# Tokens woven over partitions in steps of two, and longer runs in the DRAM turns, in a one-layer hybrid decoder

## The chip, the cores and the metric

The kernel runs on one core of one Trainium2 chip, in a single launch. The metric is the time of that launch on the device in microseconds (us); a lower one is better. The kernel before took 1533.48 us, the median of three runs that spread from 1532.01 to 1534.3.

## The reference

One decoder layer over 256 tokens of 2048 channels, in float32. Cut to what matters here:

```python
h = rmsnorm(x, norm_mix_w)                              # 256 x 2048
q, k, v, z, b, a, p_in, g_a, g_b = split(h @ w_in)      # 16 heads of 128
q, k, v = silu(causal_dwconv(concat(q, k, v), conv_w))  # 4 taps over tokens, one filter per channel
o = gated_delta_rule(l2norm(q), l2norm(k), v, g(a), sigmoid(b))
y_a = rmsnorm(o) * silu(z)
y_b = (multiscale_pool(p_in) @ pool_w) * pool_scale     # trailing means over 2, 4, 8, 16 tokens
x = x + (sigmoid(g_a) * y_a + sigmoid(g_b) * y_b) @ w_out
h = rmsnorm(x, norm_ffn_w)
gate, up = split(h @ w_up)                              # 2 x 5632 columns
gate = causal_dwconv(gate, conv_ffn_w) + conv_ffn_b     # 3 taps over tokens
x = x + (gelu(gate) * up) @ w_down
return rmsnorm(x)
```

## The kernel before

**The products.** `gemm_a` (line 356) computes 256 tokens by 512 columns. The activations are the loaded (stationary) operand, 128 channels by 128 tokens; the weights stream past them, 512 columns at a time. Activations and weights are each held as two float32r halves (`xhi`, `xlo`; `whi`, `wlo`), and a block is the sum of hi·hi, lo·hi and hi·lo. So a weight tile (`raw`, 256 channels by 512 columns, 512 KB) takes 12 matmuls: 8 with its `whi`, 4 with its `wlo`. The activations are `xhl` in the first half (q, k, v, pooled input, z and the two gates), `mhi`/`mlo` before the output projection, `fhl` before gate and up, `hhi`/`hlo` before the down projection. A block leaves in PSUM with tokens on partitions: `ps[:, t, :]` holds tokens 128t to 128t+127. `evict` (line 667) and `evicted` (line 1224) scale it by each token's norm factor (`rs1`, `rs2`: one number per partition and half) into a buffer `ev` or `fev`.

**The weight pipeline.** SyncE (its queue is called SP) loads the raw tile into one of five buffers, ScalarE (ACT) rounds it to `whi` (`cast`), VectorE (DVE) forms `wlo` (`split`). `whi` and `wlo` have four buffers each, so ACT and DVE can be at most about three tiles ahead of TensorE (PE). A raw tile is loaded when the split five tiles earlier is done.

**Turning a block.** The convolutions and the pooling run along tokens, so tokens must lie along the free dimension. `flip` (line 376) transposes 32x32 blocks on DVE (`tn`), writes them with four DMAs into a DRAM tensor `d` [512 channels, 256 tokens], and `flipped` loads that back with channels on partitions (`kq`, `vT`, `pu`, `gs`, `us`, ...). A 32x32 block row is 32 tokens, so a contiguous run in DRAM is 32 elements, 128 bytes. `flip` is used for k, q, v and the pooled input of each of four groups of heads, for the mixed output of each group (`sz` to `mhi`/`mlo`), for the four residual blocks (`xt` to `fhl`), and for 11 gate and 11 up blocks. `flip_back` (line 398) takes v back to tokens on partitions (`tb`, `back`, `vt`), again in runs of 32.

**The order.** Nothing is scheduled by hand or by the compiler: side work is written as generators ("threads"), and a planner (`Plan`, line 32) that keeps an estimated time for each engine decides after every few matmuls which thread moves on. `piece` picks a step when its operands are due, `pipeline` a load, a cast or a split. The DMA estimate (line 55) sets due times, 170 bytes per ns for runs of 32 elements and 380 for others. So a change of an estimate, or of the number of instructions of a step, moves instructions on all engines. Engines then execute in that fixed order.

**The groups.** Four groups of four heads pass through the first half, overlapped: the small products of a group's delta rule (`gdn`, line 718) are put between the weight matmuls of its gates and of the next group. The ones that matter below: from tile `lb`, 31 steps on DVE give `tb`, which goes through DRAM (`tbd`) to `tct`; then PE (`psa<-T,ga`), ACT (`U`) and DVE (`T`, `TT`) alternate. DVE also forms the trailing sums of the pooled input (`pb`, `pa` from `pu`). After the last group, its mixed output is transposed (`tn<-sz`), turned through DRAM, and split into `mhi` and `mlo`; three blocks of the output projection start on the channels of the first groups (`early`, line 1154, 18 weight tiles), and then PE needs the last group's `mhi` and `mlo`.

Of the kernel before, what the change touches and what calls it, by code (L numbers as in the profile page):

```python
# [13 lines left out]
P = 128  # L14
S = 256
# [16 lines left out]
class Plan:  # L32
# [75 lines left out]
def kernel(  # L108
# [264 lines left out]
        return ps  # L373


    def flip(pool, src, of, rank):
        yield "V", -2
        yield from take("tn")
        b = pool.tile([P, 2, 512], F32, tag="tn", name=nm("tn"))
        if of is None:  # L380
            for t in range(2):
                nc.vector.transpose(b[:, t, :], src[:, t, :])
        else:
            nc.vector.transpose(b.rearrange("p t f -> p (t f)"), src.rearrange("p t f -> p (t f)"))
            give(of)
        yield "S"
        d = dpool.tile([512, S], F32, tag="flip", bufs=4, name=nm("flip"))
        dv = d.rearrange("(f i) (t a j) -> a i t f j", i=32, t=2, j=32)
        for a in range(4):
            nc.sync.dma_start(dv[a], b[32 * a : 32 * a + 32].rearrange("p t (f j) -> p t f j", j=32))  # L390
        give("tn")
        yield "S", rank
        return d

    def flipped(dst, d):
        nc.sync.dma_start(dst, d.rearrange("(f p) s -> p f s", p=P))

    def flip_back(pool, src, dst, of):
        yield "V"
        yield from take("tn")  # L400
        b = pool.tile([P, 4, S], F32, tag="tn", name=nm("tb"))
        nc.vector.transpose(b.rearrange("p h s -> p (h s)"), src.rearrange("p h s -> p (h s)"))
        give(of)
        yield "S"
        d = dpool.tile([S, 512], F32, tag="back", name=nm("back"))
        dv = d.rearrange("(n i) (h a j) -> a i h n j", i=32, h=4, j=32)
        for a in range(4):
            nc.sync.dma_start(dv[a], b[32 * a : 32 * a + 32].rearrange("p h (n j) -> p h n j", j=32))
        give("tn")
        yield "S"  # L410
        nc.sync.dma_start(dst.rearrange("p t h d -> p t (h d)"), d.rearrange("(t p) c -> p t c", p=P))

    mix = tc.tile_pool(name="mix", bufs=1)
    mp = mix.__enter__()
# [66 lines left out]
    def xl(k, t):  # L481
        return xlo[:, k, t * P : (t + 1) * P]

    NV = 16 + KF
    V_FFN, V_CB = 0, 16
    vec = cpool.tile([P, NV], F32, name="vec")
# [3 lines left out]
    dtb = mp.tile([P, NH], F32, name="dtb")  # L490
    gwb = mp.tile([P, P], F32, name="gwb")
    rs1 = cpool.tile([P, 2], F32, name="rs1")
    rsh = cpool.tile([P, 2], F32, name="rsh")
    mats = mp.tile([P, 5, P], F32, tag="TT", name="mats")
    low, tri, ntri, ntail, top = (mats[:, i, :] for i in range(5))
# [15 lines left out]
    def norms():  # L511
        ssq4 = cpool.tile([P, 2, 4], F32, tag="ssq4", name="ssq4a")
        for c in range(4):
            for t in range(2):
                yield "A"
                plan.at(max(plan.ready, x0[c][1]))
                junk = cpool.tile([P, 512], F32, tag="sqj", name=nm("junk"))
                nc.scalar.activation(junk, x0[c][0][:, t, :], AF.Square, accum_out=ssq4[:, t, c : c + 1])
        yield "V"
        ssq = cpool.tile([P, 2], F32, name="ssq")  # L520
        nc.vector.tensor_reduce(ssq, ssq4, axis=mybir.AxisListType.X, op=ALU.add)
        rstd(ssq, rs1)
        normed.append(True)
        yield "V"
        nc.vector.tensor_scalar(rsh, rs1, 0.5, None, op0=ALU.mult)

    def vectors():
        yield "A"
# [189 lines left out]
    def gdn(g, kq, vts, dec0, dec1, res):  # L718
# [85 lines left out]
        nc.gpsimd.memset(TTa, 0.0)  # L804
        while not vts:
            yield
        vt = vts[0]
# [29 lines left out]
        for t in range(2):  # L837
            yield "A"
            for h in range(4):
                nc.scalar.activation(vt[:, t, h, :], vt[:, t, h, :], AF.Copy, scale=nk[:, t, h : h + 1])  # L840
        yield "PE"
        px = []
        for hp in range(2):
# [36 lines left out]
        w2 = mp.tile([P, 4, P], F32, tag="w2", name=nm("w2"))  # L880
        pw = pa([P, 4, P])
        for h in range(4):
            mm(pw[:, h, :], TT[h // 2][:, 0, h % 2, :], vt[:, 0, h, :], start=True, stop=True)
        yield "A"
        nc.scalar.copy(w1, pw)
        yield "PE"
# [4 lines left out]
        nc.vector.tensor_tensor(vt[:, 1], vt[:, 1], pr, op=ALU.subtract)  # L891
        yield "PE"
        pw = pa([P, 4, P])
        for h in range(4):
            mm(pw[:, h, :], TT[h // 2][:, 1, h % 2, :], vt[:, 1, h, :], start=True, stop=True)
        give("vt")
        yield "A"
        nc.scalar.copy(w2, pw)
# [109 lines left out]
    def mixing(g, sz, ps, psb, tb, res, mh, ml):  # L1008
        yield "V"
        nc.vector.scalar_tensor_tensor(tb, tb, 1.0, ps, op0=ALU.add, op1=ALU.mult)  # L1010
        yield "V"
        nc.vector.tensor_tensor(tb, tb, psb.unsqueeze(1).to_broadcast([P, 2, 512]), op=ALU.mult)
        give("psb")
        while len(res) < 2:
            yield
        plan.at(max(plan.ready, res[1]))
        yield "V"
        nc.vector.tensor_tensor(sz, sz, tb, op=ALU.add)
        give("th")
        d = yield from flip(mp, sz, "sz", g)  # L1020
        raw = ml.bitcast(F32)
        flipped(raw, d)
        yield "A"
        nc.scalar.copy(mh, raw)
        yield "V"
        nc.vector.tensor_tensor(ml, raw, mh.bitcast(F32), op=ALU.subtract)

    def gates(g):
        e = evict(gemm_a(xh, xl, KD))
# [34 lines left out]
    for g in range(4):  # L1064
# [33 lines left out]
        def values(e, g=g, vts=vts):  # L1098
            d = yield from flip(mp, e, "ev", g)
            yield from take("vT")  # L1100
            vT = mp.tile([P, 4, S], F32, tag="vT", bufs=1, name=nm("vT"))
            yield from conv_silu(d, 2, g, vT)
            yield "V"
            yield from take("vt")
            vt = mp.tile([P, 2, 4, P], F32, tag="vt", name=nm("vt"))
            yield from flip_back(mp, vT, vt, "vT")
            vts.append(vt)
            vts.append(plan.ready)

        if g == 0:  # L1110
            for k2 in range(8):
                plan.at(x0[k2 // 2][1])
                spawn(x_turned(k2), k2 - 20)

            def x_next(c):
                until(lambda: len(turned) > c)
                if c == 0:
# [8 lines left out]
            ps = gemm_a(xh, xl, KD, before=x_next)  # L1126
            pba = pa([P, 2, S])
            for c in range(2):
                hi, lo = weights()
                for kk in range(8):  # L1130
                    k = 8 * c + kk
                    mm(pba, hi[:, kk, :], xhl[:, k], start=(k == 0), stop=(k == KD - 1))
                side()

            def start(pba=pba, heads=heads):
                yield from strengths(pba)
                yield from heads()
        else:
            ps = gemm_a(xh, xl, KD)
        spawn(keys(evict(ps)), g)  # L1140
        if g == 0:
            spawn(start(), -1)
        spawn(queries(evict(gemm_a(xh, xl, KD))), g)
        if g:
            spawn(heads(), g)
        spawn(values(evict(gemm_a(xh, xl, KD))), g)
        if g:
            gates(g - 1)
    gates(3)
# [14 lines left out]
    ssq4 = cpool.tile([P, 2, 4], F32, tag="ssq4", name="ssq4b")  # L1164
    ssq2 = cpool.tile([P, 2], F32, name="ssq2")
    rs2 = cpool.tile([P, 2], F32, name="rs2")

    high = []
    squared = []

    def residual(c, ps):
# [5 lines left out]
        else:  # L1177
            nc.vector.tensor_tensor(xs, xs, ps, op=ALU.add)
        spawn(squares(c, xs), 0)
        d = yield from flip(fp, xs, None, 0)  # L1180
        ks = slice(4 * c, 4 * c + 4)
        raw = flo[:, ks, :].bitcast(F32)
        flipped(raw, d)
# [11 lines left out]
    def squares(c, xs):  # L1195
# [5 lines left out]
        if len(squared) == 4:  # L1201
            yield "V"
            nc.vector.tensor_reduce(ssq2, ssq4, axis=mybir.AxisListType.X, op=ALU.add)
            rstd(ssq2, rs2)
            squared.append(4)

    for c in range(4):
# [5 lines left out]
        spawn(residual(c, ps), 0)  # L1213

    def fh(k, t):
        return fhi[:, k, t * P : (t + 1) * P]

    def fl(k, t):
        return flo[:, k, t * P : (t + 1) * P]

    def fh_made(c):
        until(lambda: len(high) > c // 2)
# [1 line left out]
    def evicted(ps):  # L1224
# [2 lines left out]
        take_now("fev")  # L1227
        e = fp.tile([P, 2, 512], F32, tag="ev", name=nm("fev"))
        for t in range(2):
            nc.scalar.activation(e[:, t, :], ps[:, t, :], AF.Copy, scale=rs2[:, t : t + 1])  # L1230
        return e

    hhi = []
# [192 lines left out]
```

## Time and profile before

| what | value |
|---|---|
| median of three runs | 1533.48 us (1532.01 to 1534.3) |
| the profiled execution: its time, its span | 1536.53 us, 1533.5 us |
| mean granted TensorE clock in it | 0.997 |
| busy in the span: DVE, ACT, POOL | 69%, 51%, 4% |
| HBM read, written | 315.40 MB, 29.39 MB |
| DMA packets, of these under 512 B | 399271, 231190 |

The profile shows one execution, engine by engine. Its own time is 1536.53 us, of which 1533.5 are the span from the first to the last instruction; the profiled execution is 3.05 us longer than the median of the runs. In rows of the profile a name such as `psm<-whi,xhl` gives what an instruction writes and reads; PEld is the loading of the stationary operand, which overlaps PE's matmuls; SPq is SyncE's issuing of DMAs. Line 94 is a helper through which all instructions are recorded, so groups are told apart by tile.

### The profile page before, as it was taken

The page shows a single profiled execution, that of the slowest core. Times are in us where ns is not written, and L with a number is a line of the kernel's source. Part 1 is how long each engine was busy: PE and PEld are TensorE (multiplying, and loading weights), DVE is VectorE, ACT ScalarE, POOL GpSimd, SP SyncE. Part 2 cuts the span into 40 slices and gives each one's busy share as a digit, 9 for nine tenths or more (in the row PEclk, how much of TensorE's full clock was granted, in tenths as well). Part 3 has the DMA queues.
Part 4 walks back from the last instruction along what each step waited for, and adds up shares of the span by engine and source line. Part 5 has one row for each costly group of instructions (what it writes and reads, how often), then busy time and mean ns, then how long its engine had stood idle before and what let it go on. Part 6 is the DMA issues. An engine that isn't in the chain of part 4 may idle for free.

```text
span 1533.5 us, 19655 instructions
## 1 busy us (share of the span) xinstructions
PE 1519.9 (99%) x7110; PEld 1250.0 (82%) x7110; DVE 1059.4 (69%) x1525; ACT 775.4 (51%) x1023; POOL 62.5 (4%) x85
## 2 busy tenths in 40 slices
PE   9999999999999999999999999999999999999997
PEld 8887888777878887888888888888888888888886
DVE  5767878787887779885566766666666666444445
ACT  7475474466545854464455544444454444333343
POOL 1001001100010002000000000000000000000000
PEclk9999999999999999999999999999999999999999
DMA  8888975898578966974798888877887788666663
GB/s 292 224 238 219 256 243 149 206 260 256 159 178 245 288 201 167 264 230 143 228 281 270 235 255 245 258 220 242 253 248 227 237 255 240 204 193 192 220 194 108
DMA packets 399271, 346.09 MB, mean 226 GB/s; under 512 B 231190, under 2 KB 258374, under 8 KB 399174
## 3 DMA queue, kind: packets, MB, share of 16 engines
q1 hardware_dynamic: 395744, 339.32, 75.3%
q10 hardware_dynamic: 3430, 5.53, 1.1%
q8 instruction: 55, 0.90, 0.2%
q14 instruction: 42, 0.34, 0.1%
HBM read 315.40 MB, written 29.39 MB: 225 GB/s over the span
## 4 chain that ended last, share of the span: by engine, by line
PE 93%; DMA 3%; DVE 2%; issue 1%; SPq 0%; ACT 0%; POOLq 0%; POOL 0%; ACTq 0%; DVEq 0%
PE psm L94 79%; PE psa L94 8%; PE psb L94 6%; DMA raw<-in_w_in_dram 2%; DVE wlo L94 1%; DMA lb<-cdd 0%; DMA pu<-flip 0%; SPq L94 0%; DVE tmp L94 0%; ACT whi L94 0%; DVE tb L94 0%; DMA flip<-tn 0%; ACT xt L94 0%; DVE pb L94 0%; DVE tn L94 0%
## 5 line engine op out<-in xcount | busy, mean ns | idle before, releaser
L94 DVE TENSOR_TENSOR wlo<-raw,whi 128x1024 fp32r<-128x1024 f32 x524 | 635.2, 1220 | 293.1 <-ACT whi L94 291.4
L94 ACT CAST whi<-raw 128x1024 fp32r<-128x1024 f32 x526 | 549.0, 1051 | 536.9 <-PE psm L94 360.7
L94 PE MATMUL psm<-whi,xhl 128*128 128x512 f32 x1792 | 452.7, 393 | 1.4 <-ACT whi L94 1.4
L94 PEld LDWEIGHTS psm<-whi,xhl 128*128 128x128 f32 x1792 | 335.4, 188 | 71.6 <-ACT whi L94 2.2
L94 PE MATMUL psm<-whi,fhl 128*128 128x512 f32 x1408 | 347.8, 389 | 0.0
L94 PEld LDWEIGHTS psm<-whi,fhl 128*128 128x128 f32 x1408 | 264.5, 188 | 54.7
L94 PE MATMUL psm<-wlo,xhl 128*128 128x512 f32 x896 | 243.4, 394 | 0.6 <-DVE wlo L94 0.6
L94 PEld LDWEIGHTS psm<-wlo,xhl 128*128 128x128 f32 x896 | 167.4, 188 | 35.6 <-DVE wlo L94 1.1
L94 PE MATMUL psm<-wlo,fhl 128*128 128x512 f32 x704 | 188.3, 389 | 0.0
L94 PEld LDWEIGHTS psm<-wlo,fhl 128*128 128x128 f32 x704 | 132.2, 188 | 27.3
L94 PE MATMUL psm<-whi,hhi 128*128 128x512 f32 x168 | 65.4, 389 | 0.0
L94 PE MATMUL psm<-whi,hlo 128*128 128x512 f32 x168 | 65.4, 389 | 0.0
L94 ACT ACTIVATE fev<-psm,rs 128x512 f32<-128x512 f32 x44 | 27.9, 686 | 55.3 <-PE psm L94 55.3
L94 DVE STREAM_TRANSPOSE tn<-fev 128x1024 f32<-128x1024 f32 x22 | 27.4, 1244 | 32.3 <-ACT fev L94 32.1
L94 DVE SCALAR_TENSOR_TENSOR cy<-kq,cqw,cy 128x255 f32<-128x255 f32 (+2 forms) x96 | 44.5, 481 | 1.6
L94 PE MATMUL psm<-wlo,hhi 128*128 128x512 f32 x168 | 45.2, 389 | 0.0
L94 DVE SCALAR_TENSOR_TENSOR y<-gs,cfw,y 128x255 f32<-128x255 f32 x88 | 42.6, 484 | 3.1
L94 DVE TENSOR_TENSOR tmp<-lb,tb 128x248 f32<-128x248 f32 (+30 forms) x124 | 36.5, 294 | 10.1 <-DMA lb<-cdd 7.3
L94 DVE TENSOR_TENSOR tb<-tb,tmp 128x248 f32<-128x248 f32 (+30 forms) x124 | 36.9, 298 | 4.3
L94 POOL TENSOR_TENSOR rs<-ms,epsx 128x2 f32<-128x2 f32 (+1 forms) x4 | 4.2, 1062 | 822.0 <-DVE ms L94 822.0
L94 PE MATMUL psm<-whi,mhi 128*128 128x512 f32 x96 | 37.4, 389 | 0.0
L94 PE MATMUL psm<-whi,mlo 128*128 128x512 f32 x96 | 37.4, 389 | 0.0
(223 smaller groups left out, 1288.4 us busy)
## 6 DMA issues: line engine op xcount, KB each, us to landing
raw<-in_w_in_dram SPq DMA_DIRECT2D x226, 512.0 KB, 5.3
raw<-in_w_up_dram SPq DMA_DIRECT2D x176, 512.0 KB, 4.5
raw<-in_w_down_dram SPq DMA_DIRECT2D x88, 512.0 KB, 4.6
flip<-tn SPq DMA_DIRECT2D x184, 128.0 KB, 3.2
raw<-in_w_out_dram SPq DMA_DIRECT2D x32, 512.0 KB, 5.1
gs<-flip SPq DMA_DIRECT2D x11, 512.0 KB, 5.5
us<-flip SPq DMA_DIRECT2D x11, 512.0 KB, 6.2
kq<-flip SPq DMA_DIRECT2D x8, 512.0 KB, 8.2
```

Of the source, the lines that this page charges most:

```text
L94: r = getattr(self.eng, op)(out, *args, **kw)
```

## The change

- The stationary operand of the k, q, v, pooled, gate and up products takes every second token: `woven` selects tokens t, t+2, t+4, ... for half t, so partition j of `ps[:, t, :]` holds token 2j+t. The step in SBUF is 8 bytes, where it was 4. The z product and the two gate products keep the old order.
- The norm factors are needed in the same order: `rs1w` is made by four small matmuls with columns of the identity, `rs2w` by a DMA to DRAM and back (`weave`).
- `flip` has a parameter `weft`. With it (k, q, v, pooled, gate, up) each half is transposed by its own instruction into every second element of `tn`, so that 64 tokens are contiguous and the DRAM runs are 64 elements, 256 bytes. Without it (mixed output, residual) the runs stay at 32, and the mixed output's transpose too becomes two instructions.
- `flip_back` transposes head by head, and orders v's 512 columns so that a run is 128 elements, 512 bytes; `vt` has the columns in the order (a h j), and its readers view it so.
- The planner's DMA estimate gets a third rate, 250 for last dimensions of 64.

```diff
-        self.queue = max(self.queue, self.t[eng]) + n / (170e3 if out.shape[-1] <= 32 else 380e3)
+        self.queue = max(self.queue, self.t[eng]) + n / {32: 170e3, 64: 250e3}.get(out.shape[-1], 380e3)
...
+    def woven(tile, k, t):
+        return tile[:, k, :].rearrange("p (j t) -> p t j", t=2)[:, t]
+
+    def weave(out, rs):
+        yield "S"
+        d = dpool.tile([S], F32, tag="rsd", name=nm("rsd"))
+        nc.sync.dma_start(d.rearrange("(t p) -> p t", p=P), rs)
+        yield "S"
+        nc.sync.dma_start(out, d.rearrange("(p t) -> p t", t=2))
...
-    def flip(pool, src, of, rank):
+    def flip(pool, src, of, rank, weft=True):
...
-        if of is None:
+        d = dpool.tile([512, S], F32, tag="flip", bufs=4, name=nm("flip"))
+        if weft:
+            bv = b.rearrange("p t f -> p (t f)").rearrange("p (f j t) -> p f j t", t=2, j=32)
+            for t in range(2):
+                nc.vector.transpose(bv[:, :, :, t], src[:, t, :].rearrange("p (f j) -> p f j", j=32))
+            dv = d.rearrange("(f i) (a u) -> a i f u", i=32, u=64)
+            bv = bv.rearrange("p f j t -> p f (j t)")
+        else:
             for t in range(2):
                 nc.vector.transpose(b[:, t, :], src[:, t, :])
-        else:
-            nc.vector.transpose(b.rearrange("p t f -> p (t f)"), src.rearrange("p t f -> p (t f)"))
+            dv = d.rearrange("(f i) (t a j) -> a i t f j", i=32, t=2, j=32)
+            bv = b.rearrange("p t (f j) -> p t f j", j=32)
...
-        dv = d.rearrange("(f i) (t a j) -> a i t f j", i=32, t=2, j=32)
         for a in range(4):
-            nc.sync.dma_start(dv[a], b[32 * a : 32 * a + 32].rearrange("p t (f j) -> p t f j", j=32))
+            nc.sync.dma_start(dv[a], bv[32 * a : 32 * a + 32])
...
-        b = pool.tile([P, 4, S], F32, tag="tn", name=nm("tb"))
-        nc.vector.transpose(b.rearrange("p h s -> p (h s)"), src.rearrange("p h s -> p (h s)"))
+        b = pool.tile([P, 8, 4, 32], F32, tag="tn", name=nm("tb"))
+        for h in range(4):
+            nc.vector.transpose(b[:, :, h, :], src[:, h, :].rearrange("p (n i) -> p n i", i=32))
...
-        dv = d.rearrange("(n i) (h a j) -> a i h n j", i=32, h=4, j=32)
+        dv = d.rearrange("(n i) (a u) -> a i n u", i=32, a=4)
...
+    def xhw(k, t):
+        return woven(xhi, k, t)
...
+                mm(pv[64 * a : 64 * a + 64, t : t + 1], ident.rearrange("p (j t) -> p t j", t=2)[:, t],
+                   rs1[:, a : a + 1], start=True, stop=True, skip_group_check=True)
...
+        nc.vector.tensor_copy(rs1w, pv[:, 0:2])
...
-            nc.scalar.activation(e[:, t, :], ps[:, t, :], AF.Copy, scale=rs1[:, t : t + 1])
+            nc.scalar.activation(e[:, t, :], ps[:, t, :], AF.Copy, scale=rs1w[:, t : t + 1])
...
-        d = yield from flip(mp, sz, "sz", g)
+        d = yield from flip(mp, sz, "sz", g, False)
...
+            yield from weave(rs2w, rs2)
```

The change moves instructions in all four groups. Two places matter below, both on DVE, which PE waits for. The first is the delta rule of the second group, where PE's 64x64 products need the four `T` and four `TT` of DVE (32x4x32 each). Before, with `wlo` the weight splits between:

```order
L94 TENSOR_TENSOR wlo_3449<-raw_3319,whi_3412 128x1024
L94 TENSOR_TENSOR pb_3452<-pu_3398 128x4x255
L94 COPY pb_3452<-pu_3398 128x4
L94 TENSOR_TENSOR pa_3451<-pb_3452 128x4x254
L94 COPY pa_3451<-pb_3452 128x4x2
L94 TENSOR_TENSOR wlo_3470<-raw_3346,whi_3429 128x1024
L94 TENSOR_TENSOR wlo_3478<-raw_3370,whi_3476 128x1024
L94 TENSOR_TENSOR pa_3451<-pa_3451,wcnt 128x4x16
L94 SCALAR_TENSOR_TENSOR pa_3451<-pa_3451,pu_3398 128x1024
L94 TENSOR_TENSOR wlo_3533<-raw_3396,whi_3499 128x1024
L94 TENSOR_SCALAR T_3348<-psa_3539 32x4x32
L94 STREAM_TRANSPOSE TT_3349<-T_3348 32x4x32
```

And with the change, the same place from the last trailing sum on; `tcm` is the transposed `tct`, `plo` the low half of the pooled input:

```order
L94 SCALAR_TENSOR_TENSOR pa_3422<-pa_3422,pu_3382 128x1024
L94 TENSOR_TENSOR wlo_3479<-raw_3388,whi_3477 128x1024
...
L94 STREAM_TRANSPOSE tcm_3528<-tct_3469 128x256
L94 TENSOR_TENSOR wlo_3530<-raw_3408,whi_3499 128x1024
L94 SCALAR_TENSOR_TENSOR plo_3304<-pa_3422,phi_3303 128x1024
L94 TENSOR_TENSOR wlo_3545<-raw_3434,whi_3526 128x1024
...
L94 TENSOR_TENSOR wlo_3662<-raw_3553,whi_3636 128x1024
L94 TENSOR_SCALAR T_3501<-psa_3685 32x4x32
L94 STREAM_TRANSPOSE TT_3502<-T_3501 32x4x32
```

Before, three splits stand between the first sum `pb` and the first `T`, and one between the last sum `pa` and `T`; with the change nine and seven. The other place is the end of the first half, also on DVE: the transpose of the last group's mixed output (`tn<-sz`) and its `mlo`, before. The weight tile whose `wlo` is the last row is the first that PE multiplies with this `mhi` and `mlo`:

```order
L94 TENSOR_TENSOR wlo_6632<-raw_6564,whi_6630 128x1024
L94 STREAM_TRANSPOSE tn_6644<-sz_6013 128x1024
L94 TENSOR_TENSOR wlo_6652<-raw_6581,whi_6650 128x1024
L94 TENSOR_TENSOR wlo_6685<-raw_6600,whi_6675 128x1024
L94 TENSOR_TENSOR wlo_6703<-raw_6619,whi_6691 128x1024
L94 TENSOR_TENSOR wlo_6722<-raw_6638,whi_6710 128x1024
L94 TENSOR_TENSOR wlo_6741<-raw_6654,whi_6728 128x1024
L94 TENSOR_TENSOR mlo_6524<-mlo_6524,mhi_6523 128x1024
...
L94 TENSOR_TENSOR wlo_6832<-raw_6756,whi_6820 128x1024
```

With the change that first tile is the one whose split is `wlo_6869`:

```order
L94 TENSOR_TENSOR wlo_6778<-raw_6664,whi_6776 128x1024
L94 STREAM_TRANSPOSE tn_6786<-sz_6021 128x512 x2
L94 TENSOR_TENSOR wlo_6800<-raw_6699,whi_6798 128x1024
L94 TENSOR_TENSOR wlo_6832<-raw_6742,whi_6822 128x1024
L94 TENSOR_TENSOR wlo_6850<-raw_6765,whi_6838 128x1024
L94 TENSOR_TENSOR wlo_6869<-raw_6780,whi_6857 128x1024
L94 TENSOR_TENSOR wlo_6888<-raw_6802,whi_6875 128x1024
L94 TENSOR_TENSOR mlo_6460<-mlo_6460,mhi_6459 128x1024
```

Before, the split of that tile is the tenth behind the transpose, and `mlo` stands ahead of it by five; with the change it is the fourth, and `mlo` stands behind it.

More of the change, by code (lines that the diff above doesn't have):

```diff
@@ L482, in xl, with xlw @@
         return xlo[:, k, t * P : (t + 1) * P]
+    def xhw(k, t):
+        return woven(xhi, k, t)
+    def xlw(k, t):
+        return woven(xlo, k, t)
     NV = 16 + KF
@@ L492 @@
     rs1 = cpool.tile([P, 2], F32, name="rs1")
+    rs1w = cpool.tile([P, 2], F32, name="rs1w")
     rsh = cpool.tile([P, 2], F32, name="rsh")
@@ L522, in norms @@
         rstd(ssq, rs1)
-        normed.append(True)
         yield "V"
         nc.vector.tensor_scalar(rsh, rs1, 0.5, None, op0=ALU.mult)
+        yield "PE"
+        n = yield from bank()
+        pv = pb()
+        for t in range(2):
+            for a in range(2):
+                mm(pv[64 * a : 64 * a + 64, t : t + 1], ident.rearrange("p (j t) -> p t j", t=2)[:, t],
+                   rs1[:, a : a + 1], start=True, stop=True, skip_group_check=True)
+        yield "V"
+        nc.vector.tensor_copy(rs1w, pv[:, 0:2])
+        leave(n)
+        normed.append(True)
     def vectors():
@@ L806, in gdn @@
             yield
-        vt = vts[0]
+        vt = vts[0].rearrange("p t a h j -> p t h a j")
         yield "V"
@@ L882, in gdn @@
         for h in range(4):
-            mm(pw[:, h, :], TT[h // 2][:, 0, h % 2, :], vt[:, 0, h, :], start=True, stop=True)
+            mm(pw[:, h, :].rearrange("p (a j) -> p a j", a=4), TT[h // 2][:, 0, h % 2, :], vt[:, 0, h], start=True,
+               stop=True)
         yield "A"
@@ L894, in gdn @@
         for h in range(4):
-            mm(pw[:, h, :], TT[h // 2][:, 1, h % 2, :], vt[:, 1, h, :], start=True, stop=True)
+            mm(pw[:, h, :].rearrange("p (a j) -> p a j", a=4), TT[h // 2][:, 1, h % 2, :], vt[:, 1, h], start=True,
+               stop=True)
         give("vt")
@@ L1028, in gates @@
     def gates(g):
-        e = evict(gemm_a(xh, xl, KD))
+        e = evict(gemm_a(xhw, xlw, KD))
         phi = mtile(g, [P, 4, S], F32R, nm("phi"))
@@ L1104, in values @@
             yield from take("vt")
-            vt = mp.tile([P, 2, 4, P], F32, tag="vt", name=nm("vt"))
+            vt = mp.tile([P, 2, 4, 4, 32], F32, tag="vt", name=nm("vt"))
             yield from flip_back(mp, vT, vt, "vT")
@@ L1124, in x_next @@
                     spawn(matrices(), 1)
-            ps = gemm_a(xh, xl, KD, before=x_next)
+            ps = gemm_a(xhw, xlw, KD, before=x_next)
             pba = pa([P, 2, S])
@@ L1142 @@
             spawn(start(), -1)
-        spawn(queries(evict(gemm_a(xh, xl, KD))), g)
+        spawn(queries(evict(gemm_a(xhw, xlw, KD))), g)
         if g:
             spawn(heads(), g)
-        spawn(values(evict(gemm_a(xh, xl, KD))), g)
+        spawn(values(evict(gemm_a(xhw, xlw, KD))), g)
         if g:
@@ L1166 @@
     rs2 = cpool.tile([P, 2], F32, name="rs2")
+    rs2w = cpool.tile([P, 2], F32, name="rs2w")
     high = []
@@ L1179, in residual @@
         spawn(squares(c, xs), 0)
-        d = yield from flip(fp, xs, None, 0)
+        d = yield from flip(fp, xs, None, 0, False)
         ks = slice(4 * c, 4 * c + 4)
@@ L1215, in fh @@
     def fh(k, t):
-        return fhi[:, k, t * P : (t + 1) * P]
+        return woven(fhi, k, t)
     def fl(k, t):
-        return flo[:, k, t * P : (t + 1) * P]
+        return woven(flo, k, t)
     def fh_made(c):
@@ L1229, in evicted @@
         for t in range(2):
-            nc.scalar.activation(e[:, t, :], ps[:, t, :], AF.Copy, scale=rs2[:, t : t + 1])
+            nc.scalar.activation(e[:, t, :], ps[:, t, :], AF.Copy, scale=rs2w[:, t : t + 1])
         return e
```

12 lines of the change are left out of this document (6 added, 6 removed).

## The prediction

> **What bounds the kernel now.** I read the page first, then the matmul groups, then stretches of the span, then the stretch that stood out.
>
> ```profile
> span 1533.5 us, 19655 instructions
> PE 1519.9 (99%) x7110; PEld 1250.0 (82%) x7110; DVE 1059.4 (69%) x1525; ACT 775.4 (51%) x1023; POOL 62.5 (4%) x85
> DMA packets 399271, 346.09 MB, mean 226 GB/s; under 512 B 231190, under 2 KB 258374, under 8 KB 399174
> ```
>
> PE is busy for all but 13.6 us. A shorter transfer helps only where PE waits for it, so the question is where those 13.6 us lie. Stretches of PE alone (columns: length, busy, clock, DMA share, GB/s) show it:
>
> ```profile
> 0.00:20.00 20.00, 18.02 (x95) 1.00 0.90 315
> 200.00:300.00 100.00, 100.00 (x540) 1.00 0.65 180
> 300.00:400.00 100.00, 96.94 (x514) 0.98 0.84 241
> 500.00:600.00 100.00, 100.00 (x540) 1.00 0.75 221
> 1000.00:1100.00 100.00, 100.00 (x443) 1.00 0.81 238
> 1500.00:1533.50 33.50, 24.93 (x110) 0.92 0.24 86
> ```
>
> The start lacks 1.98 us and the tail 8.57; the change touches neither's work. The rest, 3.06 us, lies in 300 to 400 alone. From gate and up to the down projection (1000 to 1100 stands for it) PE runs without a gap: 443 matmuls in 100 us are 225.7 ns each, 2.71 us for a weight tile of 12. There 22 of the 38 woven flips can gain nothing. Within 300 to 400, by all engines (PE, PEld, DVE, ACT, POOL):
>
> ```profile
> 320.00:330.00 10.00, 9.76 (x44) 7.74 (x42) 8.20 (x17) 4.80 (x9) 1.36 (x2) 1.00 1.01 273
> 330.00:340.00 10.00, 9.82 (x43) 7.95 (x44) 9.32 (x23) 10.00 (x26) 0.00 (x0) 1.00 0.97 325
> 340.00:350.00 10.00, 9.37 (x42) 7.41 (x41) 8.09 (x18) 3.31 (x4) 0.00 (x0) 1.00 0.75 183
> 380.00:390.00 10.00, 7.99 (x49) 6.05 (x48) 7.56 (x14) 6.18 (x10) 0.00 (x0) 0.83 0.76 214
> ```
>
> Two troubles: 320 to 350 lacks 0.24 + 0.18 + 0.63 = 1.05 us, with the DMA engines near full; 380 to 390 lacks 2.01 us and runs at clock 0.83, another 10 x 0.17 = 1.7 us. Together 4.8 us, all that the change can find on PE.
>
> The timeline of 380 to 384 and the chain of waits before it name the second trouble:
>
> ```profile
> 382.67 0.65 PE L94 MATMUL psa<-T,ga 64*64 64x64 f32 x8 [1.35 <-DVE T L94]
> 383.97 0.65 PE L94 MATMUL psa<-T,ga 64*64 64x64 f32 x8 [0.65 <-DVE T L94]
> 366.45 7.59 DMA pu<-flip
> 374.06 1.31 DVE pb L94 x2
> 381.52 0.28 DVE L94 TENSOR_SCALAR T<-psa 32x128 f32<-32x128 f32 x1
> ```
>
> DVE, in order, waits for `pu` until 374.06; the sums and splits queued behind it make `T` late, and PE waits 1.35 + 0.65 us. For the first, SP's timeline:
>
> ```profile
> 299.94 8.86 SPq L94 DMA_DIRECT2D back<-tb  x4
> 314.31 8.87 SPq L94 DMA_DIRECT2D flip<-tn  x4
> 323.29 2.50 SPq L94 DMA_DIRECT2D raw<-in_w_in_dram  x4
> 340.10 3.04 SPq L94 DMA_DIRECT2D flip<-tn  x4
> ```
>
> Four flip writes keep SP 8.87 us where 3.04 would do later, and four raw loads come late behind them.
>
> **The change part by part.** The loads of the stationary operand come first, since 16 blocks of the first half and 22 of gate and up step, 38 x 96 = 3648 loads.
>
> ```profile
> L94 PEld LDWEIGHTS psm<-whi,xhl 128*128 128x128 f32 x1792 | 335.4, 188 | 71.6 <-ACT whi L94 2.2
> L94 PEld LDWEIGHTS psm<-whi,fhl 128*128 128x128 f32 x1408 | 264.5, 188 | 54.7
> L94 PEld LDWEIGHTS psb<-q,ones 128*32 128x32 f32 x32 | 0.6, 108 | 1.4 <-issue 1.4
> ```
>
> 96 more columns take 80 ns more, 0.83 ns each, over some 81 ns that are fixed. No row shows a step of 8 bytes. Below: no gain, for the load is hidden behind the matmul already. Above: if every column cost twice, a load would take 188 + 107 = 295 ns, 69 more than the 225.7 of a matmul, and 3648 x 69 ns = 252 us would follow. I take zero: the load has 225.7 - 188 = 38 ns of room, in which a small penalty would not be seen. [...]
>
> DVE: one transpose of 1024 becomes two of 512.
>
> ```profile
> L94 DVE STREAM_TRANSPOSE tn<-ev 128x1024 f32<-128x1024 f32 x16 | 19.8, 1239 | 4.1 <-ACT ev L94 4.1
> L94 DVE STREAM_TRANSPOSE tn<-xt 128x512 f32<-128x512 f32 x8 | 5.2, 688 | 2.2 <-DMA flip<-tn 2.2
> L94 ACT ACT_TABLE_LOAD x8 | 10.3, 1283 | 3.2 <-DMA dec<-rund 3.1
> ```
>
> 2 x 688 against 1239 is at most +0.14 us for a flip; writing every second element, which no row shows, between nothing and a doubling (+1.2 us). DVE is busy 69% and up to three splits ahead, which covers it; without that cover 16 flips of the first half would cost 2 to 19 us. I take zero. ACT gets two more table loads, 1283 ns each, and has half its time free.
>
> The flips' writes: half as many runs. The four take SP 3.04 us when nothing is queued, so between nothing and 1.5 us are saved each; v's way back, of the same size and with a quarter of the runs, between nothing and 2.3. In 300 to 330 one of each ran, so up to 3.8 us of crowding go. I take half of the first trouble: **-0.5 us** (0 to -1.05).
>
> The second trouble goes by the order: seven splits now stand between the last sum and `T`, where one stood, so DVE catches up before PE asks. At 2.71 us a tile this is 16 us more room than a delay of a few us needs; `pu` may be as late as before. **-3.7 us** (2.01 + 1.7). What is late next there is the split pair between the two `T` halves; its price is tenths.
>
> `rs1w`: four matmuls, a copy, and the first `evict` waits for them.
>
> ```profile
> 29.07 0.74 POOL L94 TENSOR_TENSOR rs<-ms,epsx 128x2 f32<-128x2 f32 x1 [23.18 <-DVE ms L94]
> 37.85 0.33 PE L94 MATMUL psb<-ident,cqrows 96*128 96x96 f32 x2
> 44.23 1.07 PE L94 MATMUL psb<-id,bat 64*128 64x32 f32 x8
> 816.52 1.64 POOL L94 TENSOR_TENSOR rs<-ms,epsx 128x2 f32<-128x2 f32 x1 [91.34 <-DVE ms L94]
> L94 ACT ACTIVATE fev<-psm,rs x44: 681/686/691, 845.0 to 1286.2; 128x512 f32<-128x512 f32 x44
> ```
>
> `rs1` is there at 29.8, and the four stand one weight tile ahead of `cqrows`, so PE waits for nothing: four of the eight `bat` are **+0.5 us**. `rs2w` needs two DMAs between 818.2 and 845.0; even 8 us each would fit. SP waits for the first to land with weight loads behind it, and two of those are let past first; PE has three tiles ahead, 8 us, to cover that.
>
> The end of the first half is where the new order takes room away. Before, from the timelines of DVE and SP and the chain:
>
> ```profile
> 716.03 2.84 PE L94 MATMUL psa<-w,ga 128*128 128x128 f32 x24
> 734.77 1.24 DVE L94 STREAM_TRANSPOSE tn<-sz 128x1024 f32<-128x1024 f32 x1
> 750.94 1.22 DVE L94 TENSOR_TENSOR mlo<-mlo,mhi 128x1024 fp32r<-128x1024 f32 x1 [2.49 <-ACT mhi L94]
> 768.77 10.88 PE psm L94 x48
> ```
>
> `mlo` is ready at 752.16 and PE asks at 768.77: 16.6 us of slack. With the change four splits stand between the transpose and PE's first use where ten stood: 6 x 2.71 = 16.3 us less. That leaves 0.3 us, with a DMA round trip in between that can go either way by a few us. I take **+0.5 us** (0 to 5).
>
> New small waits where the other groups' products have been moved: **+0.3 us**; the first and the third group showed none before (200 to 300, 500 to 600).
>
> The sum is -0.5 - 3.7 + 0.5 + 0.5 + 0.3 = -2.9 us: 1533.6 for the profiled execution's 1536.53, and from the median, 3.05 us below that execution, **1530.6 us**.
>
> **The rivals.** *Nothing gained*: new waits of the same size arise elsewhere in the first half, since the planner only guesses; 1532 to 1535. For it: the old order was as carefully guessed and failed at one place. *The last group's turn becomes the wait* (slower): `mlo` comes late by more than its 0.3 us. It decides from there; a stall of 4 us, as with a flip of 8.87 us in place of 3.04 at this place, and the clock with it, +1.7 us as at 380 to 390, give 1530.6 - 0.5 + 5.7 = 1535.8. Against it: DMA is less crowded there than at 314. On the clock, the row says that 2.0 us of waiting in two pieces went with 0.83 over 10 us. [...] *The step slows the loads*: from a penalty of over 38 ns on, up to 1530.6 + 252 = 1783 us. Against it only the room of 38 ns. *The runs gain nothing*, the DMA engines being bound by bytes: then the first trouble stays and 1531 remains, within the forecast.
>
> **How the numbers follow.** My forecast with its own spread (both troubles gone or half gone, 1528.5 to 1532) has 0.60, nothing gained 0.20, the late turn 0.14, the slow loads 0.06. About 0.2% (3.1 us) is what a measurement of this kernel tells from no change, so the edges are 1530.4 and 1536.5. Of the forecast's 0.60, 0.36 lie below 1530.4 and 0.24 within; of nothing gained 0.16 lie within, and 0.04, with more than one new wait, beyond 1536.5; of the late turn 0.08 within and 0.06 beyond; of the slow loads all beyond. Faster 0.36, same 0.48, slower 0.16. The lower end is the 4.8 us that can be found, less a half for what the runs vary: 1528.2. The upper end, 1537.5, takes in the late turn at its dearest.
>
> **What would show it.** Loads of `psm<-whi,xhl` and `fhl` still near 188 ns and 443 matmuls in 100 us show that the step is free; a PE spacing above 226 ns proves me wrong by far. The stretch 300 to 400 should have PE busy above 99.5 at clock 1.00, and no wait `psa <- DVE T` above 0.5 us. At the start of the output projection's second part, a wait of PE for `mlo` is the late turn. Flip packets should halve in number with no change in gate and up, and transposes cost 1.3 us for a flip in two.

## The result and the profile after

The changed kernel takes **1553.91 us** (median of four runs, 1553.84 to 1554.64); the kernel before took 1533.89 on the same chip (1532.01 to 1536.91). The ratio is 1.0127 (95% interval 1.0115 to 1.0139), that is 19.5 us slower by the ratio and 20.0 by the two medians. The forecast was 1530.6, with a range that ended at 1537.5. The profiled execution took 1554.64 us, its span is 1552.9. One execution among all those below is far off and is left out of the ratios: the first of the kernel with the plain first half took 3117.74 us, 2.04 times the median of its ten others, although its recorded clock was 1.00, for a reason that no run shows.

The page of the changed kernel:

```profile
span 1552.9 us, 19728 instructions
PE 1542.6 (99%) x7118; PEld 1269.5 (82%) x7118; DVE 1070.1 (69%) x1580; ACT 778.4 (50%) x1025; POOL 65.5 (4%) x85
DMA packets 309577, 346.12 MB, mean 223 GB/s; under 512 B 137398, under 2 KB 168678, under 8 KB 309478
```

PE was busy 1519.9 us, and is now busy 1542.6. So the time did not go into waiting; it went into PE's own work. The stretches of PE (length, busy, count of matmuls, clock, DMA share, GB/s) say the same:

```profile
200.00:300.00 100.00, 100.00 (x533) 1.00 0.64 183
300.00:400.00 100.00, 100.00 (x467) 1.00 0.85 253
500.00:600.00 100.00, 100.00 (x537) 1.00 0.74 218
1000.00:1100.00 100.00, 100.00 (x430) 1.00 0.81 238
```

The 3.06 us of idle time in 300 to 400 are gone, and the clock there is 1.00. But where gate and up run without a gap, 100 us hold 430 matmuls instead of 443, at the same clock. All that PE waits for, in the whole span, is this (us in total, times, longest):

```profile
PE psa L460 <- POOL ones L94: 1.0, 1, 1.0
PE psm L94 <- ACT whi L94: 0.4, 1, 0.4
PE psb L94 <- DMA nmrows<-in_norm_mix_w_dram: 0.3, 1, 0.3
```

No line names `T`, `mlo`, `rs1w` or `rs2w`: none of the waits that the prediction weighed is there. The groups of the loads of the stationary operand (count, then busy us and mean ns of one):

```profile
L94 PEld LDWEIGHTS psm<-whi,xhl 128*128 128x128 f32 x1792 | 341.0, 191 | 70.4 <-ACT whi L94 0.6
L94 PEld LDWEIGHTS psm<-whi,fhl 128*128 128x128 f32 x1408 | 271.7, 193 | 56.8
L94 PEld LDWEIGHTS psm<-whi,hhi 128*128 128x128 f32 x168 | 31.5, 188 | 6.5
```

`fhl` is always stepped, `xhl` in 16 of 28 blocks, `hhi` never: 193, 191 and 188 ns. The 5 ns look harmless beside a matmul of 226. They are not, as the starts of successive matmuls show. Two rows of PE's timeline in gate and up, first of before, then of the changed kernel (start and length in us; x4 are four matmuls):

```profile
1009.78 1.07 PE L94 MATMUL psm<-wlo,fhl 128*128 128x512 f32 x4
1010.69 1.07 PE L94 MATMUL psm<-whi,fhl 128*128 128x512 f32 x4
```

```profile
1009.95 1.09 PE L94 MATMUL psm<-wlo,fhl 128*128 128x512 f32 x4
1010.89 0.86 PE L94 MATMUL psm<-whi,fhl 128*128 128x512 f32 x3
```

Four matmuls take 0.91 us, and with the step 0.94. As a mean over the trace, 226.7 ns lie between the starts in gate and up of before, and in the blocks of its first half that no small product interrupts (such as the three from 134 to 199 us); in the changed kernel 233.3 ns in gate and up and in the uninterrupted woven blocks of the first half (the one from 87 to 110 us has 235.6), and still 226.7 in z and the gates (183 to 227 and 644 to 688 us) and in the output projection behind 778 us. Within one kernel and one execution, the stepped blocks alone are slower. At 6.67 ns for each of 3648 loads the price is 24.3 us. The spans differ by 1552.9 - 1533.5 = 19.4; so 4.9 us were gained elsewhere, near the 4.8 that the prediction had found in 300 to 400.

### The profile page after: what moved, and what is told of

Same layout as the page of the kernel before. It is cut to its first block, busy times and chain, and to the rows that moved or that the text cites. A ratio compares the mean times of both kernels' runs of the same rounds, so it can differ in the third digit from the quotient of the medians.

```text
span 1552.9 us, 19728 instructions
## 1 busy us (share of the span) xinstructions
PE 1542.6 (99%) x7118; PEld 1269.5 (82%) x7118; DVE 1070.1 (69%) x1580; ACT 778.4 (50%) x1025; POOL 65.5 (4%) x85
## 4 chain that ended last, share of the span: by engine, by line
PE 99%; issue 1%; DMA 0%; ACT 0%; POOLq 0%; DVE 0%; POOL 0%; ACTq 0%
PE psm L94 85%; PE psa L94 8%; PE psb L94 6%; DMA nmrows<-in_norm_mix_w_dram 0%; PE psa L460 0%; ACT xt L94 0%; POOLq L1461 0%; ACT whi L94 0%; POOL rs L94 0%; ACT xhl L94 0%; DVE xt L94 0%; ACTq L94 0%; DVE ms L94 0%
## 5 line engine op out<-in xcount | busy, mean ns | idle before, releaser
L94 PEld LDWEIGHTS psm<-whi,xhl 128*128 128x128 f32 x1792 | 341.0, 191 | 70.4 <-ACT whi L94 0.6
L94 PE MATMUL psm<-whi,fhl 128*128 128x512 f32 x1408 | 356.8, 394 | 0.0
L94 PEld LDWEIGHTS psm<-whi,fhl 128*128 128x128 f32 x1408 | 271.7, 193 | 56.8
L94 PEld LDWEIGHTS psm<-wlo,xhl 128*128 128x128 f32 x896 | 170.8, 191 | 34.8
L94 PE MATMUL psm<-wlo,fhl 128*128 128x512 f32 x704 | 192.5, 394 | 0.0
L94 PEld LDWEIGHTS psm<-wlo,fhl 128*128 128x128 f32 x704 | 135.9, 193 | 28.4
L94 ACT ACTIVATE fev<-psm,rs2w 128x512 f32<-128x512 f32 x44 | 27.9, 685 | 57.9 <-PE psm L94 57.9
L94 DVE STREAM_TRANSPOSE tn<-fev 128x512 f32<-128x512 f32 x44 | 28.7, 692 | 29.6 <-ACT fev L94 27.5
```

The source lines that it names most:

```text
L94: r = getattr(self.eng, op)(out, *args, **kw)
```

## The experiments

The theory after the result: **the step of 8 bytes in the stationary operand costs 6.67 ns for each load and is the whole loss; all else in the change gains about 4 us**. The rivals: the loss comes from the weave's other work (split transposes, factors through DRAM, the new order), and the gain comes from fewer packets or from the order.

### The step alone

Before, with `woven` in `gemm_a`'s operands and nothing else:

```diff
-        return fhi[:, k, t * P : (t + 1) * P]
+        return woven(fhi, k, t)
...
-        e = evict(gemm_a(xh, xl, KD))
+        e = evict(gemm_a(xhw, xlw, KD))
```

> The kernel before with one thing changed: the stationary operand of q, k, v, pooled, gate and up takes every second token (3648 loads). Tokens come out in another order, which nothing repairs here. Theory (each stepped load lengthens the spacing of its matmul by 233.3 - 226.7 = 6.7 ns): 3648 x 6.7 = 24 us more, 1554 to 1558 us, less where the slower pace swallows the old waits at 320 to 390 us; LDWEIGHTS 193 ns, spacing 233 ns. Rival (the step is free; the 64-element transposes, or the packets of 256 bytes, slow PE): 1534 us, LDWEIGHTS 188 ns.

Measured: 1553.89 us (1553.84 to 1554.12) against 1534.17, ratio 1.0127 (1.0110 to 1.0144), the changed kernel's time. Its loads of `fhl` and its stretches of PE:

```profile
L94 PEld LDWEIGHTS psm<-whi,fhl 128*128 128x128 f32 x1408 | 271.7, 193 | 56.8
```

```profile
380.00:390.00 10.00, 10.00 (x84) 1.00 0.62 165
1000.00:1100.00 100.00, 100.00 (x430) 1.00 0.80 240
```

The step alone does it. The row of 380 to 390 holds a trap: this kernel has before's order, and the wait for `T` has gone all the same. PE is slower in each woven matmul (430 in 100 us in place of 443), and what was late for it is now in time. So a gain in this stretch says nothing about the change while PE is slowed; only a kernel without the step can tell.

### The change without the step

The changed kernel, instruction for instruction in the same order, with contiguous operands:

```diff
     def woven(tile, k, t):
-        return tile[:, k, :].rearrange("p (j t) -> p t j", t=2)[:, t]
+        return tile[:, k, t * P : (t + 1) * P]
```

> The changed kernel with one thing undone: the stationary operand is contiguous again, in the same order of instructions; flips, runs, v's way back, the norm factors and the planner stay as changed. Token order is not repaired. Theory: 1553.9 - 24 = 1529 to 1530 us, with no wait of PE for T at the second group and PE full from 300 to 400 us, that is 4 us better than before. Rival (runs or transposes slow PE): stays at 1554 us.

Measured: 1530.01 us (1529.74 to 1530.29, seven runs), ratio 0.9971 (0.9960 to 0.9982). From the profile:

```profile
span 1528.2 us, 19728 instructions
```

```profile
L94 PEld LDWEIGHTS psm<-whi,xhl 128*128 128x128 f32 x1792 | 334.6, 188 | 70.1 <-ACT whi L94 0.7
L94 PEld LDWEIGHTS psm<-whi,fhl 128*128 128x128 f32 x1408 | 264.4, 188 | 54.8
```

```profile
300.00:400.00 100.00, 100.00 (x499) 1.00 0.82 242
1000.00:1100.00 100.00, 100.00 (x443) 1.00 0.83 246
```

The same 19728 instructions take 24.7 us less than the changed kernel's; 3648 x 6.67 ns are 24.3. All the rest of the change gains 4.2 us.

### The weave without a step in the load

Two ways to keep gate and up woven and their loads contiguous. In the first, tokens are interleaved in blocks of 32, and the residual's turn, now with eight writes, lays them down so:

```diff
-            dv = d.rearrange("(f i) (t a j) -> a i t f j", i=32, t=2, j=32)
+                dv = d.rearrange("(f i) (b t c j) -> c b i t f j", i=32, b=2, t=2, c=2)
...
-        return woven(fhi, k, t)
+        return fhi[:, k, t * P : (t + 1) * P]
```

> The changed kernel, but gate and up have their tokens interleaved by blocks of 32, laid down in that order by the residual's turn, so that their 2112 loads are contiguous while their runs in DRAM stay at 64 elements and their transposes stay two. Theory: 2112 x 6.7 = 14 us less, 1540 us; in gate and up 443 matmuls in 100 us as before, LDWEIGHTS of fhl 188 ns, of stepped xhl still 193. Rival (64-element runs or transposes of 512 slow PE): 1554 us and 430 matmuls in 100 us.

Measured: 1541.80 us (1541.65 to 1544.44), ratio 1.0052 (1.0037 to 1.0067). The loads of `fhl` are back at 188 ns, but in the profiled execution, the longest of the four (1544.44), there is a new wait. Its size, its place on PE, and ACT's timeline ahead of it:

```profile
PE psm L94 <- ACT whi L94: 3.4, 2, 2.5
```

```profile
841.36 3.68 PE L94 MATMUL psm<-whi,fhl 128*128 128x512 f32 x8 [2.47 <-ACT whi L94]
```

```profile
838.66 1.71 ACT L94 ACTIVATE fhl<-fhl,vec 128x256 fp32r<-128x256 f32 x4 [9.29 <-DMA fhl<-flip]
```

ACT waits 9.29 us for the last residual block, and the next `whi` stands behind that. The other three executions took 1541.65 to 1541.80; how much of this wait is in them no profile shows. In the second way the residual's turn is left as in the changed kernel, and the two instructions that round the activations read every second token, from the idle buffers of `y` and `gs`:

```diff
-        raw = flo[:, ks, :].bitcast(F32)
...
+        raw = fp.tile([P, 4, S], F32, tag=tag, name=nm("rawx"))
         flipped(raw, d)
+        raw = raw.rearrange("p k (j t) -> p k t j", t=2)
...
-            nc.scalar.activation(fhi[:, k, :], raw[:, k - 4 * c, :], AF.Copy, ...
+            nc.scalar.activation(halves(fhi, k), raw[:, k - 4 * c], AF.Copy, ...
```

> The changed kernel, but gate's and up's activations are laid down in the woven order when they are rounded (ScalarE and VectorE read every second token there, from a buffer of their own), so that their 2112 loads are contiguous. The first half keeps its 1536 stepped loads. If the step in the load alone is the price: 1530.0 + 1536 x 6.67 ns = 1540.3 us, with 226.7 ns between the matmuls of gate and up and 233.3 in q, k, v and pooled. If the weave costs in another way too (the factors' way through DRAM, the stepped reads of ScalarE and VectorE before gate), up to 1543 with waits at 800 to 850. If the load's step were not the cause, 1553.9 would stay.

Measured: 1539.92 us (1539.59 to 1540.07), ratio 1.0032 (1.0019 to 1.0044), where 1540.3 was expected:

```profile
L94 PEld LDWEIGHTS psm<-whi,xhl 128*128 128x128 f32 x1792 | 341.0, 191 | 70.5 <-ACT whi L94 0.8
L94 PEld LDWEIGHTS psm<-whi,fhl 128*128 128x128 f32 x1408 | 264.3, 188 | 54.8
```

```profile
1000.00:1100.00 100.00, 100.00 (x443) 1.00 0.80 235
```

So the weave itself costs nothing that can be seen in the time: the same permutation, taken where ACT and DVE read instead of where PE loads, takes ACT 517 ns an instruction in place of 500, and DVE 480 in both kernels, 16 instructions each. What is left of the loss is the first half's 1536 loads, 10.2 us at 6.67 ns (1539.92 - 1530.01 = 9.9 measured), whose operand `xhl` is needed in both orders.

### What the step is charged by

Three ladders: before, with the operand of each column block of gate and up (192 matmuls) read in another way, by one line like this (`flat` is `fhl` as one row, `at` the usual start plus an offset in elements):

```diff
-        return fhi[:, k, t * P : (t + 1) * P]
+        return flat[:, at : at + P * step].rearrange("p (j u) -> p u j", u=step)[:, 0]
```

> The kernel before with the loads of gate and up at other steps, one step for each of the 11 column blocks in turn: 1, 2, 3, 4, 5, 6, 8, 16, 1 with an offset of one element, 2, 1 (128 elements from the activation buffer, so other values are multiplied). What a load costs is read from LDWEIGHTS and the matmul spacing of each block. [...] Theory B (any step but one pays a fixed price): 233 ns at all steps. [...]

> The kernel before; the eleven column blocks of gate and up (192 matmuls each) read their stationary operand in eleven ways, so other values are multiplied there. In order, step and offset in elements: (1,0), (1,1), (1,2), (1,3), (1,4), (1,8), every second load at step 2 and the others at 1, (2,1), (7,0), (12,0), (1,0). If each load is charged by itself, the sixth way gives 230.0 ns between matmuls on the mean; if a stepped load disturbs its neighbours, 233. If the price is one for whatever is not whole and aligned, offsets 1 and 3 cost 5.6 ns as offset 1 did, offsets 4 and 8 nothing, and offset 2 tells whether 8 or 16 bytes must be met; step 2 at offset 1 then costs no more than step 2. [...]

> The kernel before; gate's and up's eleven column blocks read their stationary operand, other values than the reference's, at step and offset (1,0), (1,16), (1,32), (1,48), (1,64), (1,96), (1,120), (2,64), (9,0), (24,0), (1,0). If a contiguous load is charged for not starting on some boundary of 64, 128 or 256 bytes, the offsets 16, 32 or 64 and 96 are free again (226.7 ns). If it is charged for lying in two pieces of 512 bytes, all offsets from 16 to 120 cost the 6.6 ns of offset 8. If the price follows the spread of the addresses over the memory, step 24 costs as step 12 or 8 did and step 9 as step 7 (239).

They took 1550.72, 1553.19 and 1549.85 us (one run each). Between the starts of successive matmuls lay, as a mean over a block, from the trace (elements of 4 bytes; the load's own mean behind it):

```
step  1   offset 0         226.7 ns   load 188
step  2   offset 0, 1, 64  233.3      193
step  3, 4, 5, 6           235.5, 235.0, 236.7, 237.8   253, 310, 300, 306
step  7, 8, 9              238.8, 244.4, 243.3          311, 329, 329
step 12, 16, 24            268.2, 235.2, 253.3          366, 300, 351
step  1   offset 1, 2, 3, 4       232.4, 230.7, 231.6, 233.2   188, 188, 188, 189
step  1   offset 8, 16            233.3, 233.3                 188
step  1   offset 32, 48, 64       232.4, 228.9, 226.8          188
step  1   offset 96, 120          232.4, 233.3                 188
steps 1 and 2 in turn      230.0      187 and 194
```

Rows of the first ladder's profile behind it, the loads of steps 2, 3 and 8, each from its own stretch:

```profile
L94 PEld LDWEIGHTS psm<-whi,fhl 128*128 128x128 f32 x103 | 19.9, 193 | 4.1
```

```profile
L94 PEld LDWEIGHTS psm<-whi,fhl 128*128 128x128 f32 x111 | 26.4, 253 | 0.0
```

```profile
L94 PEld LDWEIGHTS psm<-whi,fhl 128*128 128x128 f32 x114 | 29.2, 328 | 0.0
```

Five things follow. On the mean each load is charged by itself: steps 1 and 2 in turn give 230.0, the mean of 226.7 and 233.3. The recorded length of a load is no measure of the charge: at step 4 it is 310 ns, longer than the 235.0 between matmuls, and a contiguous load at offset 8 has its 188 ns and is charged 6.6. Of the contiguous loads tried, those at offsets 0 and 64 alone are free (226.7 and 226.8 ns), which start at multiples of 256 bytes from the start of the tile; the ten other offsets are charged 2.2 to 6.6 ns, so it is not the gap between the elements as such. The start is not all either: the value of offset 3 is a mean of two, 233.2 ns over its first 96 matmuls and 229.9 over the other 96, whose loads have the same starts. And the theory of one price for all that is not whole and aligned falls too: steps 7 to 12 and 24 cost more, up to 41.5 ns at step 12, in no simple order (16 costs no more than 3).

### Where the 4 us come from

First v's way back alone, on the kernel before; the lines are `flip_back`'s and those of the readers of `vt`:

```diff
-        nc.vector.transpose(b.rearrange("p h s -> p (h s)"), src.rearrange("p h s -> p (h s)"))
+        for h in range(4):
+            nc.vector.transpose(b[:, :, h, :], src[:, h, :].rearrange("p (n i) -> p n i", i=32))
...
-        dv = d.rearrange("(n i) (h a j) -> a i h n j", i=32, h=4, j=32)
+        dv = d.rearrange("(n i) (a u) -> a i n u", i=32, a=4)
```

> Only v's way back is changed: runs of 128 elements, and four transposes where there was one. No load is stepped, the weave is absent. If what was gained in 300 to 400 comes from fewer packets, v's way back is a part of it, and 1532 to 1533 us follow. If it comes from the order of the instructions on VectorE, that order is here moved by three more transposes a group, and the stall may go (1530) or stay (1534). The loads stay at 188 ns and 226.7 ns between matmuls in every case.

Measured: 1535.61 us (1534.50 to 1536.99, eleven runs) against 1534.61, ratio 1.0006 (0.9997 to 1.0015), no change. Its stretches:

```profile
320.00:330.00 10.00, 10.00 (x46) 1.00 0.96 284
330.00:340.00 10.00, 10.00 (x46) 1.00 0.85 241
340.00:350.00 10.00, 10.00 (x46) 1.00 0.94 262
370.00:380.00 10.00, 8.52 (x66) 1.00 0.53 172
380.00:390.00 10.00, 7.60 (x43) 0.66 0.69 181
```

The first trouble is gone entirely, with v's way back alone. PE comes earlier by that, and the wait for `T` takes it back: 3.88 us of idle time in 370 to 390, 3.2 of them for `T`, where before had 2.01. The clock suffers more as well: the trace's record of the granted clock has half the clock for 3.41 us in before, from 384.69 on, and for 6.83 us here, from 381.75 on. Then the order alone, on the kernel before: two transposes, and the planner's rate, with every run in DRAM as it was:

```diff
-            nc.vector.transpose(b.rearrange("p t f -> p (t f)"), src.rearrange("p t f -> p (t f)"))
+            for t in range(2):
+                nc.vector.transpose(b[:, t, :], src[:, t, :])
...
+        plan.turn = 250e3 if of == "ev" else 170e3
```

> The kernel before; the flips of q, k, v and pooled are transposed by two instructions in place of one, and the planner counts them at the rate for runs of 64. All runs in DRAM stay as before, nothing is woven. On VectorE seven splits stand between the last trailing sum and T, as in the changed kernel. If the order alone takes away the wait for T, 3.7 us go: 1530 to 1531, with the small gaps of 320 to 350 (1 us) left. If fewer packets are needed for it: 1534.

Measured: 1534.40 us (1533.34 to 1535.72, eleven runs) against 1535.17, ratio 0.9997 (0.9988 to 1.0006): no change again. That is the number expected if fewer packets were needed, but not for that reason. The stretches and a place in PE's timeline:

```profile
300.00:400.00 100.00, 100.00 (x510) 1.00 0.89 251
500.00:600.00 100.00, 96.57 (x520) 1.00 0.75 223
```

```profile
549.88 1.20 PE L95 MATMUL psm<-wlo,xhl 128*128 128x512 f32 x4 [2.00 <-DVE wlo L95]
```

The order does take the second group's wait for `T` away, and also the small gaps of 320 to 350, which were expected to stay. But 3.4 us come back in the third group. DVE's timeline there:

```profile
547.40 1.22 DVE L95 TENSOR_TENSOR pa<-pu 128x1020 f32<-128x1020 f32 x1 [7.11 <-DMA pu<-flip]
```

DVE stands at a trailing sum until `pu` lands, and PE then waits for the split behind it: the wait of the second group, one group later and on another tile. Last both together, without any weave in the first half (runs of 32 there, the order as in the changed kernel, v's way back in runs of 128, gate and up woven by the rounding instructions):

```diff
-        d = yield from flip(mp, e, "ev", g)
+        d = yield from flip(mp, e, "ev", g, False)
...
-        spawn(queries(evict(gemm_a(xhw, xlw, KD))), g)
+        spawn(queries(evict(gemm_a(xh, xl, KD))), g)
```

> As the run with the laid down activations, and the first half is not woven: q, k, v and pooled in runs of 32, with the two transposes and the planner's rate for runs of 64, so that the order of the instructions is nearly that of the changed kernel. v's way back in runs of 128, gate and up in runs of 64. No load is stepped. If the gain of 4 us in 300 to 400 comes from the order: 1530.0 to 1530.5. If it comes from fewer packets in the first half: 1532 to 1534, with waits in 300 to 400 as before.

> The kernel of the run with the plain first half, for a second sample and a profile of its own: 1530 to 1532 us. In the profile PE busy over 99.5 in 300 to 400 at clock 1.00, if the order is what took the stall away there, and 226.7 ns between matmuls everywhere.

Measured the first time: 1530.89 us (ten of eleven runs from 1529.31 to 1532.47), ratio 0.9975 (0.9965 to 0.9984). The second time: 1529.96 us (1529.25 to 1531.52, ten runs), ratio 0.9973 (0.9963 to 0.9982), with this profile:

```profile
300.00:400.00 100.00, 100.00 (x507) 1.00 0.86 245
500.00:600.00 100.00, 100.00 (x540) 1.00 0.77 223
1000.00:1100.00 100.00, 100.00 (x443) 1.00 0.83 247
```

```profile
542.45 1.22 DVE L95 TENSOR_TENSOR pa<-pu 128x1020 f32<-128x1020 f32 x1 [6.81 <-DMA pu<-flip]
```

DVE waits for `pu` in the third group nearly as long as in the kernel with the order alone, but 5 us earlier, and PE has no gap there. So two parts, each worth nothing alone, are worth 4 us together: the order removes the wait in the second group, and with v's new way back the one that would follow in the third does not come. In the first half, v's way back is nearly all in which the text of this kernel differs from the one with the order alone, but the planner moves instructions on every engine with it; whether its longer runs, its split transposes or the moved order do that was not tried. This kernel has no stepped load and is faster than both kernels of the study. Turned runs of 64 in the first half add nothing to it: the change without the step, which has them, took 1530.01.

## Why the prediction was wrong

**The failed step** is "I take zero: the load has 225.7 - 188 = 38 ns of room, in which a small penalty would not be seen." The 38 ns are no room. (The 225.7 divides 100 us by a count that takes in the matmuls cut by the stretch's edges; the starts lie 226.7 ns apart.) As to the size, the planner's own estimate for these matmuls (line 66) is (512 + 32)/2400 us = 226.7 ns, as measured; for the 6.67 ns with the step it has no term. By the records a load starts some 3 ns after the start of the matmul ahead of it and ends 35 ns before its own (2.5 and 38 ns with the step), while the whole grows by 6.7. So, as far as the records go, what I called room is a part of each round, between the load and its matmul; what happens in it no row shows, and why the step is charged stays open. That "PEld overlaps PE" did not mean that a longer load is hidden: 193 ns in place of 188 went with 233.3 in place of 226.7.

**The step of 8 bytes** is charged 6.67 ns, and contiguous loads at the ten offsets tried off a multiple of 256 bytes are charged 2.2 to 6.6 ns. The load's own length grows from step to step at first (193 ns at step 2, 253 at step 3, 310 at step 4); the time between matmuls, which is what counts, hardly does (233.3, 235.5 and 235.0 ns).

**The rival** "the step slows the loads" had the right direction, with a chance of 0.06, but its condition ("from a penalty of over 38 ns on") and its price (69 ns a load) rested on the same mistake. The case between, a few ns on each of 3648 loads, was left out of the sum, although 1 ns of it is 3.6 us, more than the whole expected gain.

**The first trouble**, taken as half gone: all of its 1.05 us went, by v's way back alone, and by the order alone as well. **The second**: gone, by the order as I argued; but that alone would only have moved it to the third group.

**The last group's turn**, taken at +0.5 (0 to 5) with 0.3 us of slack. DVE's timeline and the chain of waits of the changed kernel:

```profile
772.15 1.23 DVE L94 TENSOR_TENSOR mlo<-mlo,mhi 128x1024 fp32r<-128x1024 f32 x1 [1.98 <-ACT mhi L94]
```

```profile
774.17 10.88 PE psm L94 x48
```

`mlo` is ready at 773.38 and PE asks at 774.17: 0.8 us of slack, and no wait. The count of splits was a good measure; the 16.6 us before were in fact spent. **The transposes**:

```profile
L94 DVE STREAM_TRANSPOSE tn<-fev 128x512 f32<-128x512 f32 x44 | 28.7, 692 | 29.6 <-ACT fev L94 27.5 <-DMA flip<-tn 2.1
L94 DVE STREAM_TRANSPOSE tn<-xt 128x512 f32<-128x512 f32 x8 | 5.2, 688 | 3.5 <-DMA flip<-tn 3.5
```

Two cost 1.38 us for a flip, and writing every second element costs DVE 4 ns in 690: nothing, as taken. **`rs1w`** took 0.41 us (+0.5 taken), and the new small waits are not there (+0.3 taken).

With what was measured, the sum without the step is -1.05 - 3.7 + 0.4 = -4.35 us; the change without the step shows -4.2. So the other terms were each off by 0.55 us at most, and the one that was set to zero was +24.3.

## What to carry to other kernels

In a kernel that PE bounds, multiply any doubt about the stationary load by the number of loads before you call it hidden: 6.67 ns times 3648 was five times the 4.8 us that there were to gain. If operands must be permuted, try it where ScalarE or VectorE pass over them anyway, so that PE loads contiguous rows: here that brought gate and up back from 430 to 443 matmuls in 100 us, for 17 ns on each of 16 ScalarE instructions. And when two waits follow each other, try the remedies together as well as one by one: here each alone measured as nothing (ratios 1.0006 and 0.9997), and both together as 0.9973.

## What the runs showed of the hardware

- Contiguous loads of 128 four-byte columns were charged mainly by their start: 226.7 and 226.8 ns between matmuls at the two offsets tried that are multiples of 256 bytes from the tile's start (0 and 64 elements), 228.9 to 233.3 at the ten others, with 188 to 189 ns recorded for the load in all cases. At one start (offset 3) two values were seen, 233.2 and 229.9.
- Loads that were recorded as longer than the time between matmuls (310 ns against 235.0 at step 4) did not set the pace; the charge at step 4 is 8.3 ns, hardly more than the 6.67 at step 2.
- Step 12 was dearer than step 16 (268.2 against 235.2 ns); why, no run tells.
